# A planned instruction order for a Strassen matmul with GELU: two sets of planner constants changed

## The chip, the cores and the metric

The kernel runs on one core of a Trainium2 chip. The metric is the device time of one execution in microseconds. PE is the matmul engine, PEld its weight loads, DVE the vector engine, ACT the scalar engine, POOL the engine whose queue issues the loads here, SP the one whose queue issues the stores.

## The reference

Two float32 matrices of 4096 x 4096 are multiplied, and the approximate GELU is applied to every element:

```python
def reference(a, b):
    x = np.matmul(a, b)
    return 0.5 * x * (1 + np.tanh(np.sqrt(2 / np.pi) * (x + 0.044715 * x**3)))
```

## The kernel before, in words

**The arithmetic.** The kernel multiplies in float16 with a Strassen-like scheme. A and B are cut into 2 x 2 quadrants ("11", "12", "21", "22"), and seven products P1 to P7 of sums of quadrants take the place of eight. Each half of the rows is worked in 4 blocks (`mb`) and each half of the columns in 4 (`nb`); a pair of blocks is one group, which makes 16 groups, 0 to 15. Within the products of many groups the scheme is applied once more: a product is then cut again into seven smaller ones with 256 columns (`part_pe`, line 950), where an uncut one has matmuls of 512 columns (`products`, line 558).

**What moves.** Raw B is loaded by `load_raw` and raw A by `turn_quad`, both on POOL's queue; the transfer also turns float32 into float16. A quarter-block of raw A is turned on DVE (`transpose`, line 435) and each of its rows is squared and summed on ACT (line 1201), since the kernel ends with a test on the size of its inputs; raw B is squared on ACT too (line 1235). The sums of B's quadrants are made on DVE (`combine2`, line 866), stored to DRAM as units (`k_unit`, 512 KB a quarter) and pieces of units (`k_piece`) on SP's queue, and fetched again on POOL's queue in later row blocks. So a made piece has a round trip: DVE, store, fetch, PE. Results leave PE's banks through ACT (line 963, 1155, 1161) or DVE additions (`add_bank`, line 1167; `add_part`, line 967), become GELU on ACT (`out_of`, line 1145) and are stored from small tiles `y`, of which there are 15. All DMAs of the planned part are issued at line 784. The row blocks of A change in three turns, in groups 3, 7 and 11; the last two share POOL's queue with fetches of units.

**Where the order comes from.** Group 0 (`first_group`) is written out by hand, and its DMAs are issued at lines 460 and 654. From group 1 on the kernel does not issue instructions as it goes. It adds each as an `Op` with a duration to a `Plan`: its engine, what it reads and writes, and for a transfer a `size`, taken from the table `MOVE`. `Plan.keys` gives each operation a due time from the work behind it on PE. `Plan.schedule` then walks through time with a model of the engines and of the transfers. PE takes its operations in the order in which they were added. Any other engine takes, whenever it is free, the ready operation that is due first. `Plan.next_move` lets the open transfers share one channel; a queue has at most `LANES` = 8 of them open. `Plan.emit` issues everything in the order of the planned starts. On the chip each engine runs its own list in that order, and semaphores hold an instruction until its inputs are there. The planned times themselves never reach the chip; they only set the order.

Two lines of the planner use what the change touches. A due time takes off the time of a transfer, and an operation that reads what a transfer brought is ready a little after it:

```python
    def latency(self, o):
        return 6.0 + 1.5 * o.size if o.size else o.dur
    ...
                late = 0.0 if s.eng == o.eng and not o.size else LAG
                if o.size and s.eng in ("DVE", "ACT"):
                    late += MARGIN
```

Of the kernel before, what the change touches and what calls it, by code (L numbers as in the profile page):

```python
# [64 lines left out]
    "SP": [(0.62, t) for t in (10.4, 11.2, 12.4, 13.6, 14.6, 15.4, 16.2)],  # L65
}
LAG = 0.2
MARGIN = 1.5
LANES = 8
MOVE = {"store": 1.33, "fetch": 1.42, "out": 0.66, "raw_a": 1.35, "raw_b": 0.68, "tiny": 0.2}  # L70
HEAVY = 1.8
COST = {
    "full": 0.861, "half": 0.876, "wide": 0.983,
# [56 lines left out]
class Plan:  # L130
# [70 lines left out]
    def schedule(self):  # L201
# [13 lines left out]
        def finish(o):  # L215
            for s in o.succ:
                s.left -= 1
# [3 lines that stand above are left out]
                s.ready = max(s.ready, o.end + late)  # L221
# [93 lines left out]
def half_path(  # L315
# [463 lines left out]
    def dma(queue, dst, src, r, w, what, **kw):  # L779
        eng = {"POOL": nc.gpsimd, "SP": nc.sync}[queue]  # L780
        weight = HEAVY if what == "unit" else 1.0
        if what == "unit":
            what = "fetch" if queue == "POOL" else "store"
        return plan.add(queue, COST[queue], lambda: eng.dma_start(out=dst, in_=src), r=r, w=w, size=MOVE[what],  # L784
                        weight=weight, **kw)
# [1099 lines left out]
```

## Time and profile before

| | before |
|---|---|
| time, median of 3 runs | 1508.8 us (1503.86, 1508.8, 1509.66) |
| profiled execution, its own time | 1503.99 us |
| its span, first to last instruction | 1502.3 us |
| busy: PE / DVE / ACT / POOL | 99% / 79% / 47% / 31% |
| matmuls | 9886 |
| mean granted matmul clock | 0.998 |
| moved by DMA, mean rate | 397.14 MB, 264 GB/s |
| median time to landing: unit fetched / tile out / unit stored | 7.1 / 7.7 / 8.3 us |

The span is what the profile sees, and the time of the same execution is 1.7 us longer. The busy shares are means over all groups. Group 0 and the groups of raw B (1 to 6) load from the inputs; from group 7 on B's sums are fetched. The spread of the three runs is 5.8 us, 0.4% of the time.

### The profile page before, as it was taken

To read this page: it belongs to the slowest core of one execution; us is meant where nothing else is said; L and a number is where in the kernel's file an instruction comes from. 1 tells how busy PE (TensorE), PEld (TensorE's weight loads), DVE (VectorE), ACT (ScalarE), POOL (GpSimd) and SP (SyncE) were. 2 spreads that over 40 slices of the span, in tenths; PEclk is the share of its full clock that TensorE was granted. 3 is DMA by queue.
4 is the path that set the end of the run, shared out by engine and by line. 5 is a ranking of instruction groups with operands and counts; after the bars stand their busy time and mean duration, and the time that the engine had idled before them with its cause. 6 is when DMAs were issued, how large, how long until landed. Compare 5 with 4: busy or idle time off the path is not lost.

```text
span 1502.3 us, 26267 instructions
## 1 busy us (share of the span) xinstructions
PE 1486.2 (99%) x9886; PEld 968.1 (64%) x9886; DVE 1192.5 (79%) x1458; ACT 711.2 (47%) x1611; POOL 464.4 (31%) x834
## 2 busy tenths in 40 slices
PE   9999999999999999999999999999999999999998
PEld 4444454444445546565665788887665778888886
DVE  2597667357689899887799999998699987879886
ACT  5445246365854455546663142436564234343333
POOL 7766341542105315212330212222231112321310
PEclk9999999999999999999999999999999999999999
DMA  9999799999879999978997776898998567988976
GB/s 177 196 207 224 137 282 328 276 287 259 238 252 238 286 360 243 316 211 276 254 321 278 274 249 220 316 306 204 280 294 313 179 248 260 350 305 281 355 266 226
DMA packets 203366, 397.14 MB, mean 264 GB/s; under 512 B 20576, under 2 KB 110944, under 8 KB 203232
## 3 DMA queue, kind: packets, MB, share of 16 engines
q0 software_dynamic: 141024, 238.08, 65.9%
q1 hardware_dynamic: 62064, 157.19, 27.6%
q8 instruction: 79, 1.29, 0.3%
q14 instruction: 55, 0.45, 0.1%
q10 hardware_dynamic: 144, 0.13, 0.0%
HBM read 321.92 MB, written 157.29 MB: 319 GB/s over the span
## 4 chain that ended last, share of the span: by engine, by line
PE 88%; DMA 7%; POOL 2%; DVE 1%; issue 1%; ACT 0%; DVEq 0%; POOLq 0%; ACTq 0%
PE acc L558 47%; PE acc L950 42%; DMA bR<-k_unit 2%; DMA stage<-in_a_dram 2%; DMA out_dram<-y 1%; POOL stage L460 1%; POOL bR L460 1%; DVE bR L866 1%; DMA k_piece<-bR 1%; DMA bR<-in_b_dram 1%; POOL aD L460 0%; DVE y L1167 0%; DMA aD<-in_a_dram 0%; ACT stage L469 0%; POOL bR L784 0%
## 5 line engine op out<-in xcount | busy, mean ns | idle before, releaser
L558 PE MATMUL acc<-bR,aT 128*128 128x512 f16 x1920 | 421.6, 379 | 6.6 <-DVE y L1167 3.5
L866 DVE TENSOR_TENSOR bR<-bR 128x2048 f16<-128x2048 f16 (+1 forms) x284 | 331.7, 1188 | 53.8 <-PE acc L950 24.7
L558 PEld LDWEIGHTS <-aT 128*128 128x128 f16 x1984 | 194.0, 98 | 235.0 <-issue 7.4
L784 POOL DMA_DIRECT2D bR<-k_unit x254 | 146.4, 579 | 593.6 <-PE acc L950 337.5
L950 PE MATMUL acc<-bR 128*128 128x256 f16 x2576 | 299.2, 273 | 0.0
L558 PE MATMUL acc<-bR,aD 128*128 128x512 f16 x1344 | 294.5, 379 | 0.0
L950 PEld LDWEIGHTS <-bR 128*128 128x128 f16 x2576 | 252.1, 98 | 31.5 <-issue 0.2
L558 PEld LDWEIGHTS <-aD 128*128 128x128 f16 x1440 | 140.8, 98 | 167.4 <-DVE aD L543 0.8
L1167 DVE TENSOR_TENSOR y<-acc,y 128x512 f32<-128x512 f32 x304 | 197.4, 684 | 58.3 <-PE acc L950 23.8
L784 POOL DMA_DIRECT2D bR<-in_b_dram x288 | 155.8, 547 | 250.7 <-PE acc L558 98.8
L963 ACT COPY y<-acc 128x256 f32<-128x256 f32 x220 | 81.8, 372 | 231.8 <-PE acc L950 231.6
L950 PE MATMUL acc<-bR,aT 128*128 128x256 f16 (+1 forms) x1536 | 181.9, 274 | 1.8 <-DMA bR<-k_unit 1.2
L1145 ACT ACTIVATE y<-y 128x512 f32<-128x512 f32 x192 | 115.5, 626 | 132.0 <-DVE y L1167 130.4
L950 PEld LDWEIGHTS <-aT 128*128 128x128 f16 x1536 | 150.1, 98 | 24.0 <-DMA bR<-k_unit 1.5
L1235 ACT ACTIVATE y<-bR 128x1024 bf16<-128x1024 f16 x128 | 130.3, 1052 | 58.2 <-DVE y L1240 49.8
L950 PE MATMUL acc<-bR,aD 128*128 128x256 f16 (+1 forms) x1040 | 124.5, 275 | 0.0
L950 PE MATMUL acc<-bR,stage 128*128 128x256 f16 (+1 forms) x1008 | 120.3, 274 | 0.0
L950 PEld LDWEIGHTS <-aD 128*128 128x128 f16 x1040 | 102.5, 99 | 15.0
L950 PEld LDWEIGHTS <-stage 128*128 128x128 f16 x1008 | 98.7, 98 | 16.7
L1240 DVE TENSOR_TENSOR y<-y 128x1024 bf16<-128x1024 bf16 x120 | 82.1, 685 | 22.9 <-ACT y L1235 21.5
L1201 ACT ACTIVATE y<-bR 128x512 f16<-128x512 f16 x128 | 80.5, 629 | 26.0 <-DMA bR<-in_a_dram 22.5
L866 DVE TENSOR_TENSOR bR<-aT 128x2048 f16<-128x2048 f16 x61 | 74.0, 1217 | 20.0 <-PE acc L558 16.7
(92 smaller groups left out, 1220.5 us busy)
## 6 DMA issues: line engine op xcount, KB each, us to landing
bR<-k_unit POOLq DMA_DIRECT2D x254, 512.0 KB, 7.1
out_dram<-y SPq DMA_DIRECT2D x251, 256.0 KB, 7.7
k_unit<-bR SPq DMA_DIRECT2D x112, 512.0 KB, 8.3
bR<-in_b_dram POOLq DMA_DIRECT2D x384, 128.0 KB, 7.0
k_piece<-bR SPq DMA_DIRECT2D x44, 512.0 KB, 5.1
bR<-k_piece POOLq DMA_DIRECT2D x40, 512.0 KB, 7.8
bR<-in_a_dram POOLq DMA_DIRECT2D x64, 256.0 KB, 7.9
stage<-in_a_dram POOLq DMA_DIRECT2D x48, 256.0 KB, 7.5
```

The costliest lines, as they stand in the source:

```text
L460: nc.gpsimd.dma_start(out=dst, in_=src)
L558: nc.tensor.matmul(acc, sa[:, j // 2, i * P : (i + 1) * P, j % 2], sb[:, j, :], start=start and j == 0, stop=stop and j == 3, skip_group_c ...
L784: return plan.add(queue, COST[queue], lambda: eng.dma_start(out=dst, in_=src), r=r, w=w, size=MOVE[what], weight=weight, **kw)
L866: nc.vector.tensor_tensor(out=dst, in0=xa, in1=ya, op=ALU.add if op > 0 else ALU.subtract)
L950: nc.tensor.matmul(PS[s][i][:, :] if wide else PS[s][i][:, w * HC : (w + 1) * HC], sa[:, j // 2, r * P : (r + 1) * P, j % 2], rhs(j, wide) ...
L963: act(cost, lambda: nc.scalar.copy(out=d, in_=x), [xt] if xt else [], [dt])
L1145: act("gelu", lambda: nc.scalar.activation(t, t, ACT.Gelu_apprx_tanh), [("f", f)], [("f", f)])
L1167: dve("add", lambda: nc.vector.tensor_tensor(out=sm(g), in0=bank(s, i), in1=sm(f), op=ALU.add), [("f", f)], [("f", g), ("p", s, i)])
L1201: act("weigh", lambda x=x, r=r, s=s, f=f: nc.scalar.activation(small[f].bitcast(F16)[:, : 2 * RUN], s[:, x, :], ACT.Square, accum_out=t[:, ...
L1235: act("square", lambda t=t, src=src: nc.scalar.activation(t, src, ACT.Square), [c(cx)], [("f", f)], slack=60.0)
L1240: dve("add16", lambda t=t, u=u: nc.vector.tensor_tensor(out=u, in0=u, in1=t, op=ALU.add), [("f", f)], [("f", e)], slack=60.0)
```

## The change

Two constants of the planner are other ones. Each transfer counts as 3% longer (all six entries of `MOVE`), and `MARGIN`, the extra time after which DVE and ACT may read what a transfer brought, goes from 1.5 to 2.0 us. No operation, no tile, no address and no code of the planner differs; what can differ is the order of the instructions on DVE, ACT and the queues of POOL and SP, from group 1 on.

```diff
 LAG = 0.2
-MARGIN = 1.5
+MARGIN = 2.0
 LANES = 8
-MOVE = {"store": 1.33, "fetch": 1.42, "out": 0.66, "raw_a": 1.35, "raw_b": 0.68, "tiny": 0.2}
+MOVE = {"store": 1.37, "fetch": 1.463, "out": 0.68, "raw_a": 1.391, "raw_b": 0.7, "tiny": 0.206}
 HEAVY = 1.8
```

## The prediction

> **What bounds the kernel now.** I read the busy line of the page first, then the waits of PE alone, then the chain of work that ended last around PE's longest waits, and last the transfers in windows.
>
> ```profile
> PE 1486.2 (99%) x9886; PEld 968.1 (64%) x9886; DVE 1192.5 (79%) x1458; ACT 711.2 (47%) x1611; POOL 464.4 (31%) x834
> ```
>
> PE is busy for 1486.2 of 1502.3 us, so 16.1 us are not matmul. Every other engine has room on average. The change can touch only those 16.1 us or add to them: the list holds the same matmuls in the same order, because PE's operations are taken in the order in which the program added them, whatever the planner's times.
>
> ```profile
> PE acc L558 <- DVE y L1167: 3.5, 2, 2.4
> PE acc L558 <- DMA bR<-k_unit: 3.1, 1, 3.1
> PE acc L567 <- DVE table L739: 1.5, 1, 1.5
> PE acc L950 <- DMA bR<-k_unit: 1.2, 1, 1.2
> PE acc L950 <- DVE y L1167: 0.5, 1, 0.5
> PE acc L593 <- DMA bR<-in_b_dram: 0.5, 1, 0.5
> PE acc L558 <- ACT y L576: 0.4, 1, 0.4
> PE acc L558 <- DVE aD L543: 0.3, 1, 0.3
> ```
>
> These are all of PE's waits: microseconds in total, how many, the longest. The rows of L567, L593, L576 and L543 (2.7 us) belong to the first group, whose order is written out and not planned; nothing in the diff reaches them. The last matmul ends at 1497.2 us by the timeline (a run of 13.98 us from 1483.24), so 5.1 us are the last activation, store and wind-down. What is left to the planner is 3.5 + 3.1 + 1.2 + 0.5 = 8.3 us: 4.0 us in which PE waits for DVE to empty a bank, and 4.3 us in which it waits for a fetched unit. 2.7 + 5.1 + 8.3 make the 16.1.
>
> The chain of work through the longest wait for a unit, and through the longest for DVE (start, us, what):
>
> ```profile
> 1028.17 1.13 DVE bR L866
> 1029.30 0.28 issue
> 1029.59 0.90 POOL bR L784 x2
> 1030.49 0.25 issue
> 1030.74 0.57 POOL bR L784
> 1031.30 10.11 DMA bR<-k_unit
> 1041.42 0.02 issue
> 1041.44 0.02 POOLq L784
> 1041.46 0.53 issue
> 1041.98 16.28 DMA bR<-k_unit
> 1058.26 0.04 issue
> 1058.31 1.89 PE acc L558 x8
> ```
>
> ```profile
> 487.75 7.28 DMA out_dram<-y
> 495.02 0.03 issue
> 495.05 0.02 DVEq L1167
> 495.07 0.04 issue
> 495.12 0.70 DVE y L1167
> 495.82 0.04 issue
> 495.86 1.02 PE acc L558 x4
> ```
>
> At 1058 a unit took 16.28 us from issue to landing, against a median of 7.1 for its row on the page, and POOL could issue it only when an earlier one had landed. At 496 DVE waited for a finished tile to leave, because the small tile that it wants to write was still being stored.
>
> **The change, part by part.** Nothing is added or removed on any engine; only the planner's picture of the future changes, and with it the order on DVE, ACT, POOL and SP.
>
> *Longer transfers.* A fetch goes from 1.42 to 1.463 in the planner's list, a store from 1.33 to 1.37, a tile out from 0.66 to 0.68. At most 8 transfers are open on a queue, so the planner sees the last of a full queue land 8 x 0.043 = 0.34 us later than it did. The due times on which it ranks move by 1.5 x 0.043 = 0.06 us only. This reorders where two candidates were nearly level, and nowhere else.
>
> Is 1.42 too short now? Two windows, each with the transfers' share and rate in its last two columns:
>
> ```profile
> 1138.70:1158.70 20.00, 20.00 (x110) 10.61 (x109) 17.87 (x22) 8.57 (x14) 2.63 (x5) 1.00 1.03 409
> 1031.00:1058.00 27.00, 24.20 (x144) 13.88 (x142) 15.85 (x23) 19.64 (x51) 9.20 (x17) 1.00 1.08 266
> ```
>
> Where only units and finished tiles move, 409 GB/s make 0.524 MB / 409 = 1.28 us for one unit: shorter than both lists. Ahead of the wait at 1058, where raw A is loaded too, the queues are as full (share 1.08) and move 266 GB/s, which would be 1.97 us for a unit: longer than both. So the new list is wrong by a little more in quiet stretches and right by a little more in the turns of A. I price it at the turns, where PE waits.
>
> [...]
>
> *Data usable half a microsecond later.* This holds for DVE and ACT behind a transfer, not for PE. It concerns the transposes of raw A (row L435), the squares of raw A and B (L1201, L1235) and the sums of fetched units (L866). The planner fills the half microsecond with another instruction where one is ready. The displaced one then runs up to one instruction later on the chip: 1.22 us behind a sum or a transpose, 0.68 us behind an addition from a bank, 0.82 us behind a square with its accumulator read on ACT. Its cover: the waiters for L435 are ACT, POOL, and PE's weight loads for 0.2 us in all, so no matmul now waits on a transpose; behind a displaced sum stands its store, and behind that a fetch. Queued behind the displaced instruction is only the rest of its own engine, with 310 us idle on DVE and 791 on ACT. I take nought for it, between -0.5 us a wait (DVE no longer stands idle for the transfer) and +1.22 us a place where cover is gone.
>
> *What becomes of the 8.3 us.* At 1058 POOL stands in order between raw loads, whose buffers come free only when L435 and L1201 have read them, and fetches. With those readers 0.5 us later in the plan and the queue 0.34 us longer, the fetch is ranked about 0.84 us better against the raw load; the wait of 3.1 becomes 2.3. Bounds: nothing gained, or all 3.1. The wait of 1.2 at 1411 hangs on a store and a fetch in a row (11.42 and 7.61 us in the chain), with PE next: I take 0.3 us off, the longer queue alone. The two waits of 3.5 us behind a tile's store lose 2 x 8 x 0.02 = 0.3 us. Sum: 0.84 + 0.3 + 0.3 = 1.4 us gained. SP's and POOL's issues (0.33 and 0.53 us each) are as many as before.
>
> **The time.** The profiled execution took 1503.99 us for its span of 1502.3. The runs shown are 1503.86, 1508.8 and 1509.66, so with the profiled one two lie near 1504 and two near 1509, and their middle is (1503.99 + 1508.8) / 2 = 1506.4, 2.4 above the profiled one. 1503.99 - 1.4 + 2.4 = 1505.0. Against the median of 1508.8, about 0.5% (7.5 us) is what a measurement of this kernel can tell from no change: faster is below 1501.3, slower above 1516.3.
>
> **The rivals.**
> - *All the planned waits go.* Fetches in the turns are ranked early enough, and DVE does other work instead of standing behind a store. Then 8.3 us go: 1506.4 - 8.3 = 1498.1. For it: the waits are few and short, and the two at 1058 and 1411 are both late transfers, which is what the change plans for. It is also the only reading under which the 5 us between the two kinds of runs, if late transfers make them, would shrink. Against it: 0.84 us of better rank does not outweigh a transfer of 16.28 us, and 4.0 us hang on small tiles of which there are no more than before. Chance 0.25.
> - *Raw loads ahead of fetches: slower.* Place: the turns of A in which units are fetched too, 690 to 800 us and around 1040. A raw half quadrant is four loads of 256 KB; at the 266 GB/s of the turn they take 4 x 0.262 / 266 = 3.9 us. If at a full queue such four get in ahead of the unit that PE needs next, that unit lands 3.9 us later. From two such places on it decides (7.9 us); three give 1506.4 + 11.8 = 1518.2. For it: POOL is in order and already waits 13.9 us for L1201 between 690 and 800; the raw loads are lengthened too, and are due earlier. Against it: the later readers of raw A hold the next raw load back. Chance 0.13.
> - *The round trip of a made piece: slower.* A sum on DVE, its store and its fetch follow each other, and at 1411 PE has no time to spare behind them. A sum displaced by a sum and an addition is 1.22 + 0.68 = 1.9 us late; six such trips without cover give 1506.4 + 11.4 = 1517.8. Against it: PE shows one such wait in 60 stored pieces. Chance 0.08.
> - *No order that matters changes*, because due times move by 0.06 us: 1506.4. Chance 0.10.
>
> **How the numbers follow.** The forecast has 0.44. Faster is the first rival, 0.25; slower the second and third, 0.21; the rest, 0.54, is the same within the bound. Both ends are unsure, so the range goes from the first rival's 1498 to the two slower ones' 1518, which leaves out their far halves, about 2 in 10. The likeliest case's own range is 1502 to 1510: the bounds of its three terms and the two kinds of runs.
>
> **What would show it.** Right: PE's busy time stays at 1486; its waits are the same two kinds, with 6 to 8 us in all in the planned part; a wait for k_unit near 1058 is still there and shorter. The first rival shows as planned waits under 2 us. The second shows as a wait of PE for k_unit of 4 us and more in 690 to 1130 with raw loads just ahead on POOL; the third as waits of PE for k_unit or k_piece behind L866 and a store, after 800 us. I am wrong if PE's waits are of a kind that the trace above does not show, or if matmuls themselves take longer.

## The result and the profile after

The changed kernel is slower by 0.87%: 1518.39 us, the median of eight runs (1513.15 to 1523.7), against 1505.35 us for the kernel before on the same chip (eight runs, 1500.54 to 1509.66). The ratio is 1.0087, with a 95% interval from 1.0061 to 1.0113. The profiled execution of after took 1515.43 us for a span of 1513.9 us, 11.6 us more than the span of before.

The engines do what they did. The busy line of the page of after:

```profile
PE 1489.0 (98%) x9886; PEld 968.6 (64%) x9886; DVE 1198.0 (79%) x1458; ACT 714.0 (47%) x1611; POOL 465.1 (31%) x834
```

The counts are the same, and so is PE's list, instruction for instruction. PE's busy time grew by 2.8 us. PE's waits grew more. Their view for after, without the rows of the first group (us in total, how many, the longest):

```profile
PE acc L558 <- DMA bR<-k_unit: 5.6, 2, 3.1
PE acc L558 <- DVE bR L866: 3.7, 1, 3.7
PE acc L950 <- ACT y L963: 3.3, 1, 3.3
PE acc L558 <- DVE y L1167: 1.9, 2, 1.1
...
PE acc L950 <- DVE bR L866: 0.7, 1, 0.7
```

All waits of PE add up to 19.6 us, against 11.0 before. Two of the large rows are of a kind that before does not have: a sum on DVE (L866, at 555 us) and a copy on ACT (L963, at 783 us). The wait for a unit at 1058 is 2.5 us instead of 3.1, the one at 1411 is gone, and a new one of 3.1 us stands at 1115.

The rest of the difference is the granted clock. Before ran at half clock for 3.41 us, behind its wait at 496. After does so for 10.24 us: 6.83 behind 555 and 3.41 behind 783 (both kernels without the stretch behind the last matmul). Four stretches of after by windows (stretch, length, then busy time and count of PE, PEld, DVE, ACT and POOL, the granted clock, and the transfers' share and rate):

```profile
550.32:553.73 3.41, 0.80 (x4) 0.28 (x3) 3.08 (x4) 2.19 (x3) 1.13 (x3) 1.00 1.02 419
553.73:557.15 3.42, 2.35 (x6) 0.84 (x6) 3.42 (x4) 0.00 (x0) 3.20 (x6) 0.50 1.05 338
...
779.01:782.42 3.41, 0.36 (x4) 0.18 (x2) 2.03 (x2) 0.75 (x3) 1.06 (x2) 1.00 1.04 410
782.42:785.84 3.42, 3.13 (x15) 2.16 (x15) 3.42 (x6) 3.30 (x10) 0.00 (x0) 0.50 1.01 412
```

In each pair PE has little to do in the first stretch (0.80 and 0.36 us busy), and the clock of the next one is 0.50. At half clock a matmul of 512 columns follows the one before it after 0.42 us (behind 555) and one of 256 columns after 0.21 us (behind 783 and behind before's 496). At full clock the same kernels take 0.22 and 0.11 us for it. From these steps I estimate the cost at 2.8 us behind 555, at 1.4 us behind 783, and at 1.6 us behind before's wait at 496. So the waits grew by 8.6 us and the half clock by 2.8 + 1.4 - 1.6 = 2.6 us. Together that is 11.2 of the 11.6 us.

**Where the wait at 783 comes from.** The timeline of ACT around it, after (start, us, what, and in brackets the idle time and who ended it):

```profile
776.02 0.63 ACT L963 COPY y<-acc 128x256 f32<-128x256 f32 x2
781.67 0.63 ACT L1201 ACTIVATE y<-bR 128x512 f16<-128x512 f16 x1 [5.02 <-DMA bR<-in_a_dram]
...
782.30 0.63 ACT L963 COPY y<-acc 128x256 f32<-128x256 f32 x2
```

The same place before:

```profile
767.96 0.63 ACT L1201 ACTIVATE y<-bR 128x512 f16<-128x512 f16 x1 [2.55 <-DMA bR<-in_a_dram]
...
774.59 0.37 ACT L963 COPY y<-acc 128x256 f32<-128x256 f32 x1 [0.37 <-PE acc L950]
775.47 0.37 ACT L963 COPY y<-acc 128x256 f32<-128x256 f32 x1 [0.50 <-PE acc L950]
```

ACT stands for 5.02 us at a square of raw A whose data land at 781.5 us, and the two copies that free PE's banks are behind that square in its list; they start at 782.30, when it is through. In before the squares stand ahead of the copies too. There the load landed at 767.8 us, and the copies waited for PE, not PE for them. The last load of raw A was issued 7.3 us later (766.4 against 759.1) and took 15.1 us instead of 8.7. Four fetches stand earlier on POOL's queue than in before: one has got ahead of the half quadrant before it, two in among that one's loads, and one ahead of the last half quadrant itself. That they are what made it late is read from the order; it was not tried.

**Where the wait at 555 comes from.** The timeline of DVE in group 5, after:

```profile
537.84 6.90 DVE L866 TENSOR_TENSOR bR<-bR 128x2048 f16<-128x2048 f16 x6 [0.79 <-DMA bR<-in_b_dram]
...
550.65 0.69 DVE L1240 TENSOR_TENSOR y<-y 128x1024 bf16<-128x1024 bf16 x1 [0.52 <-ACT y L1235]
551.26 6.89 DVE L866 TENSOR_TENSOR bR<-bR 128x2048 f16<-128x2048 f16 x6
```

The same six sums before:

```profile
544.45 6.89 DVE L866 TENSOR_TENSOR bR<-bR 128x2048 f16<-128x2048 f16 x6
```

The sums that PE needs begin at 551.26, 6.8 us later than in before. The first of them reads a load that landed at 549.2. Ahead of them DVE and ACT take turns at the squares of raw B, and before those stands an earlier block of six sums. The raw B quadrants that feed this place land later than in before: the first of its batch was issued at 485.8 instead of 482.2 us, and two of its loads, the second of them the last, landed at 537.6 and 549.2 instead of 526.9 and 541.3. The first eight loads of the batch overwrite a buffer that a sum in group 4 reads. That sum runs 6.0 us later than in before (first line before, the others after):

```profile
477.97 1.22 DVE L866 TENSOR_TENSOR bR<-bR 128x2048 f16<-128x2048 f16 x1
...
479.13 0.69 DVE L1257 TENSOR_REDUCE stat_b<-y 128x16 f32<-128x512 bf16 x1
...
484.01 1.21 DVE L866 TENSOR_TENSOR bR<-bR 128x2048 f16<-128x2048 f16 x1
```

In after a statistics operation of raw B (lines 1255 to 1257) is on DVE in its place, and by the instruction lists another sum and three additions have come ahead of it too. Five of the loads behind the eight were then overtaken by eight others with the same due time. Of the kernels below (without e8_doses, whose order is planned anew) only e3_groups1to6 and e6_after_square have this exchange in their lists, and only these two have the wait at 555. This beginning of the chain is read from the lists; it was not tried by itself.

**Where the wait at 1115 comes from.** Two steps of the chain of waits, after:

```profile
1099.49 15.34 DMA bR<-k_unit
1114.83 0.04 issue
1114.87 3.18 PE acc L558 x14
```

In before this fetch was issued at 1090.4 us and took 7.6 us. Here it was issued 9.1 us later and took twice as long.

### The profile page after: what moved, and what is told of

It is laid out like the page before. It is cut to its first block, busy times and chain, and to the rows that moved or that the text cites. A ratio compares the mean times of both kernels' runs of the same rounds, so it can differ in the third digit from the quotient of the medians.

```text
span 1513.9 us, 26246 instructions
## 1 busy us (share of the span) xinstructions
PE 1489.0 (98%) x9886; PEld 968.6 (64%) x9886; DVE 1198.0 (79%) x1458; ACT 714.0 (47%) x1611; POOL 465.1 (31%) x834
## 5 line engine op out<-in xcount | busy, mean ns | idle before, releaser
L866 DVE TENSOR_TENSOR bR<-bR 128x2048 f16<-128x2048 f16 (+1 forms) x284 | 331.1, 1188 | 48.6 <-PE acc L950 21.3
L963 ACT COPY y<-acc 128x256 f32<-128x256 f32 x220 | 81.5, 372 | 225.1 <-PE acc L950 220.9
L967 DVE TENSOR_TENSOR acc<-acc,y 128x256 f32<-128x256 f32 x220 | 85.0, 424 | 12.0 <-ACT y L963 5.6
L1161 ACT COPY y<-acc 128x512 f32<-128x512 f32 x84 | 48.4, 588 | 97.1 <-PE acc L558 58.8
```

Of the source, the lines that this page charges most:

```text
L866: nc.vector.tensor_tensor(out=dst, in0=xa, in1=ya, op=ALU.add if op > 0 else ALU.subtract)
L963: act(cost, lambda: nc.scalar.copy(out=d, in_=x), [xt] if xt else [], [dt])
L967: dve("part", lambda: nc.vector.tensor_tensor(out=d, in0=xa, in1=ya, op=ALU.add), [xt, yt], [dt])
L1161: act("copy", lambda: nc.scalar.copy(out=sm(f), in_=bank(s, i)), [], [("f", f), ("p", s, i)])
```

## The experiments

Ratios are against the kernel before on the same chip, with a 95% interval. The medians of before were 1507.44 us beside the first four runs, 1506.1 beside the next four and 1506.18 beside the last four.

**One constant at a time.**

```diff
# e1_margin
-MARGIN = 1.5
+MARGIN = 2.0
# e2_moves
-MOVE = {"store": 1.33, "fetch": 1.42, ...
+MOVE = {"store": 1.37, "fetch": 1.463, ...
```

> Only the later use of landed data (MARGIN 2.0), transfers as before. Theory A (the time sits in three placed waits of PE, at 555, 783 and 1115 us of the changed kernel, with the half clock behind them; the one at 555 needs both constants, because raw B's loads must be late and be swapped): no wait over 2 us at 555, a wait of ACT and so of PE near 783 is possible; 1505 + 3 to 6 us, so 1508 to 1511. Rival B (the half microsecond alone does it all): all three waits, 1518. Rival C (no place: everything a little later everywhere): 1512, with no single wait that is new and over 2 us.

> Only the transfers 3% longer, MARGIN as before. Theory A: none of the three waits, 1505 within 3 us, the waits of PE in all within 2 us of the 11.0 of the kernel before. Rival B: 1505. Rival D (the longer transfers do it all): all three waits, 1518. Rival C: 1512, no single new wait over 2 us.

The longer transfers alone do nothing: 1507.98 us, 1.0004 [0.9986, 1.0023], waits of 10.2 us, and no half clock before the end (mean granted clock 0.999, against 0.998 in before with its one stretch). The later data alone cost as much as the whole change within the intervals: 1519.2 us, 1.0075 [1.005, 1.01]. My theory had 1508 to 1511 for it and missed. The waits of PE in e1_margin show one row that carries it:

```profile
PE acc L950 <- ACT y L963: 10.8, 3, 5.9
```

It has no wait at 555. Instead PE waits for ACT's copies at 778 (4.4 us) and at 1144 (5.9 us), in the turns of raw A in groups 7 and 11, and behind each the clock is at half for 3.41 us. So a part of the change costs by waits that the whole change does not have.

**New constants for some groups only.** An operation counts by its number in the plan:

```diff
+NEW = range(0, 2137)     # e3: groups 1 to 6; e4: 2137 on (groups 7 to 15); e5: 343 on (groups 2 to 15)
-                    late += MARGIN
+                    late += MARGIN if o.n in NEW else 1.5
...
-size=MOVE[what]
+size=(MOVE if len(plan.ops) in NEW else MOVE_WAS)[what]
```

> Both new constants for the operations of groups 1 to 6 alone, the old ones from group 7 on. Theory A: the wait at 555 is there (3 to 5 us, and 3.4 or 6.8 us at half clock behind it, 1.7 to 3.4 us more), those of 783 and 1115 are not; 1505 + 5 to 7 = 1510 to 1512. Rival C: 6 of 15 groups of a loss of 13 us spread evenly: 1510.5, but without a wait over 2 us that the kernel before has not.

> The other half: the old constants for groups 1 to 6, both new ones from group 7 on. Theory A: no wait at 555; the wait near 783 (3.3 us and 1.4 behind it, on ACT's copies) and the one near 1115 (3.1 us, on a fetched unit) are there: 1505 + 5 to 8 = 1510 to 1513. Rival C: 1513 without new waits over 2 us. Rival E (the later waits are only pushed on by what happened at 555): 1505, neither wait.

> Both new constants everywhere but in group 1, which keeps the old ones. Theory A2 (the loss is a few waits of PE that an early shift of the order sets up; the wait at 555 needs both constants from group 1 on): no wait over 2 us at 555, 5 to 7 us less than the changed kernel, 1512, and 1507 if the last raw half quadrant of the first turn with fetches then lands early enough. Rival C (the loss is spread over all groups): group 1 is one of 15, so about 1517 to 1518.

Groups 1 to 6 alone give the whole loss: 1520.48 us, 1.0094 [1.0065, 1.0124]. Their profile has the wait at 555 (3.7 us) and also the one at 783 (4.6 us), though from group 7 on the planner has its old constants. I had expected no wait at 783 there and 1510 to 1512 us, and missed both. Groups 7 to 15 alone cost nothing: 1504.43 us, 0.9997 [0.9973, 1.0022], without the waits at 783 and 1115. Theory A had them there and missed; rival E, which had neither and no loss, fits. In e3_groups1to6 a unit is waited for at 1117 as well (2.1 us). So neither wait comes from the constants at the place where it is seen. An order that has changed early goes on changing what follows.

With the old constants in group 1 and the new ones in all others, the wait at 555 is gone, and the kernel takes 1511.94 us, 1.0023 [0.9995, 1.0051]. The median is 6.4 us below after's, which fits the 6.5 us that the wait and its half clock cost in after (3.7 + 2.8); by the ratios it is 0.64%, or 9.6 us. The wait for ACT in group 7 remains, 3.1 us at 778.7, and so do waits for units at 1064, 1112 and 1425 (3.2, 2.2 and 2.9 us).

**The squares of raw A behind PE's copies.** In these kernels ACT's list alone differs, by the squares that are moved behind the two copies in a turn of raw A: one square of group 7 in after, and twelve squares of groups 7 and 11 in e1_margin.

```diff
# e6_after_square; e7_margin_squares has twelve such pairs
-        self.schedule()
+        self.schedule(); [setattr(self.ops[x], 'start', self.ops[y].start + 1e-4 * (k + 1)) for k, (x, y) in enumerate([(2422, 2470)])]
```

> The changed kernel with one swap in ACT's list: a square of raw A (L1201) that stands ahead of two copies (L963) comes behind them. Theory A2 (PE's wait at 783 is ACT standing in order behind a raw load that lands at 781.5, and nothing else): the wait of 3.3 us and the half clock of 1.4 us behind it go, 1518 - 4 to 5 = 1513 to 1514, all other waits stay. Rival F (PE waits there for something that is late anyway): the wait stays within 1 us, 1518.

> The kernel with MARGIN alone changed (1519), with the squares that stand ahead of copies put behind them in both turns that share POOL with fetches: twelve places in ACT's list, all other lists as they were. Theory A2: both waits (4.4 and 5.9 us, with 1.4 us of half clock behind each) go: 1519 - 13 = 1506, the time of the kernel before. Rival F: within 3 us of 1519. Rival G (the next raw loads, released by squares that are later, take the waits' place): 1512.

In e7_margin_squares the whole loss of the later data is gone: 1507.79 us, 0.9994 [0.997, 1.0017]. Of the 10.8 us of PE's waits for L963 this is left:

```profile
PE acc L950 <- ACT y L963: 0.5, 1, 0.5
```

This settles the margin alone: its cost was ACT standing at a square with PE's copies behind it.

In after the same move gave less: 1516.47 us, where 1513 to 1514 was expected, 1.007 [1.004, 1.01], and its interval overlaps after's. The wait for ACT is gone, but the next run of matmuls on line 558, which waits for nothing in after, now waits for a unit, as the timeline of e6_after_square shows:

```profile
781.76 2.54 PE L558 MATMUL acc<-bR,aD 128*128 128x512 f16 x11 [1.86 <-DMA bR<-k_unit]
```

In after this late unit was hidden behind the wait for ACT. Taking one away shows the other.

**What the half clock needs.** To see how much idle time brings the half clock, I added to the kernel before one to seven copies on DVE of an operand onto itself, ahead of every eighth product, so that PE waits for them. The order is planned anew with the copies in it, so the time of this kernel is no measure of anything else.

```diff
+    def dose(i, b_cell):
+        seen[0] += i == 2
+        k = seen[0] // 8 % 7 + 1 if i == 2 and seen[0] % 8 == 0 else 0
+        for _ in range(k):
+            plan.add("DVE", 0.6, lambda: nc.vector.tensor_copy(out=cell(b_cell), in_=cell(b_cell)), w=[c(b_cell)])
...
+        dose(i, b_cell)
```

> The kernel before with made waits: ahead of every eighth product's third tile DVE copies that product's operand onto itself, 1 to 7 times in turn, and PE must wait for it. Theory H (a wait of PE costs itself, and 1.7 us more where more than about 2 us of it fall into one period of 3.413 us of a fixed grid, since the clock is then granted at half for the next period): waits under 1.8 us are never followed by the half clock, waits over 3.8 us always, those between by where they lie. Rival I (the half clock follows the length of the wait alone): one length parts all waits, wherever they lie. The order is planned anew around the added copies, so the time is no test.

The half-clock stretches of a trace start on a grid of 3.413 us: those of after at 553.73 and 782.42 lie 228.69 us apart, 67 times 3.413, and in e8_doses the first, at 150.54, and the one at 1345.21 lie 1194.67 us apart, 350 times 3.413. I cut the trace along that grid and read PE's idle time in each period as its length less PE's busy time. Two pairs of periods, by windows of e8_doses:

```profile
447.50:450.92 3.42, 1.36 (x7) 0.39 (x4) 3.35 (x5) 0.79 (x2) 0.00 (x0) 1.00 0.70 261
450.92:454.33 3.41, 2.49 (x6) 0.87 (x7) 3.38 (x5) 0.00 (x0) 0.00 (x0) 0.50 0.00 0
...
1160.89:1164.30 3.41, 1.44 (x7) 0.68 (x7) 0.00 (x0) 3.25 (x10) 1.06 (x2) 1.00 1.03 414
1164.30:1167.72 3.42, 3.42 (x18) 1.57 (x16) 1.21 (x2) 0.36 (x2) 1.06 (x2) 1.00 1.04 416
```

An idle time of 3.42 - 1.36 = 2.06 us was followed by a period at 0.50. One of 3.41 - 1.44 = 1.97 us was not. All nineteen full-clock periods of this trace with 2.06 to 3.42 us idle were followed by half clock, and none with up to 1.97 was. In the traces of before, after, e1_margin, e7_margin_squares and e10_margin_raw_a the edge lies at the same place, between 1.97 and 2.00 us, where both outcomes were seen: 1.97 us was followed by half clock in e10_margin_raw_a, 1.97 us in e1_margin and 2.00 us in e7_margin_squares were not.

**The forecast's own place.** In before, the fetch that PE waits for at 1058 and two behind it are put ahead of five later-due loads on POOL's queue:

```diff
+        ... for k, (x, y) in enumerate([(3529, 3520), (3530, 3520), (3531, 3520), (3532, 3520), (3543, 3520)])]
```

> The kernel before with one edit in POOL's list alone: the fetch on which PE waits at 1058 (3.1 us) and the two fetches behind it go ahead of five loads that are due later and were issued first only because their buffers came free first. Theory J (that wait is made by POOL's order): the wait goes, 3.1 us and 1.7 more where it set off the half clock, 1506 - 3 to 5 = 1501 to 1503, a version that beats both. Rival K (the unit is late because raw A fills the queues, whatever the order): the wait stays over 2 us, 1506.

The wait of 3.1 us at 1058 is gone: the fetch lands at 1047.6 us, against 1058.3 in before, so POOL's order made that wait. Two stand there instead that before does not have, at 1069 and 1134:

```profile
PE acc L950 <- ACT y L963: 1.7, 1, 1.7
PE acc L950 <- ACT y L1161: 1.1, 1, 1.1
```

The time is 1503.46 us, 0.9981 [0.9963, 1.0000]: a gain at the edge of what was measured. It is the lowest median of all kernels here, and the only one whose interval does not reach above 1.

**Whose margin it is.** The margin of 2.0 for the readers of raw A alone, and for all other readers alone, each against the old list of transfers:

```diff
# e10_margin_raw_a
-                    late += MARGIN
+                    late += MARGIN if o.size == MOVE["raw_a"] else 1.5
# e11_margin_rest
-                    late += MARGIN
+                    late += 1.5 if o.size == MOVE["raw_a"] else MARGIN
```

> MARGIN 2.0 for the readers of raw A alone (transposes and squares), 1.5 for all others, transfers as before. Theory L (the half microsecond adds up along the chain load, readers, next load of a turn, and the last half quadrant comes late): it lands at 771 us and later against 767.8 in the kernel before, PE waits for ACT's copies near 778 and 1143 as with MARGIN alone, 1515 to 1519. Rival M (raw A comes late because the whole order around it is shifted, readers of units and raw B too): less than 2 us of waits there, 1506 within 3.

> The complement: MARGIN 2.0 for all readers but those of raw A. Theory L: no wait of PE for ACT's copies in the turns, 1506 within 3 us. Rival M: one or both of those waits, 1510 to 1519.

The waits for ACT's copies came as expected: 2.8 us at 784 and 3.6 us at 1146 with the readers of raw A, none over 0.5 us with the others. The rows, of e10_margin_raw_a and of e11_margin_rest:

```profile
PE acc L950 <- ACT y L963: 7.0, 3, 3.6
...
PE acc L558 <- DMA bR<-k_unit: 7.0, 2, 4.2
```

The second row was not expected: with the others, PE waits 4.2 us for a unit at 774, and the clock is at half for 6.83 us around it. The times did not follow the waits: 1509.8 us, 1.0022 [1.0003, 1.0042], where 1515 to 1519 was expected, and 1506.74 us, 1.0019 [0.9998, 1.0039]. Their sum, 0.4%, is less than e1_margin's 0.75%, whose two waits were each some 1.6 times as long (4.4 and 5.9 against 2.8 and 3.6 us). How the two parts lengthen each other's waits was not followed further.

**Both causes out.** The kernel with the old constants in group 1, and in it two squares of group 7 behind the copies:

```diff
# e5_groups2to15, and:
+        ... for k, (x, y) in enumerate([(2422, 2470), (2423, 2470)])]
```

> Both new constants from group 2 on (1511.9 with the old ones in group 1), and two squares of raw A put behind the two copies that PE needs in the first turn with fetches: the two large waits of the changed kernel are both taken away. Theory A2: 1512 - 3.1 - 1.4 = 1507.5; what is then left above the kernel before (2 us) are waits for fetches near 1112 and 1424. Rival N (the wait only moves to the fetch behind it, as when the square alone was moved in the changed kernel): 1510 to 1511.

It takes 1510.35 us, 1.0031 [1.0014, 1.0048], where theory A2 had 1507.5. The wait for ACT in group 7 is gone from its profile, but the time is not below that of e5_groups2to15 by anything that the intervals tell. So what the wait for ACT costs the whole change is read from its trace, 3.3 us and 1.4 of half clock; neither e6_after_square nor e12_both is faster than the same kernel with it by more than the noise. Late units remain, 2.9 us at 1059 and 2.2 us at 1105, and the tile's wait at 496 (2.2 us). The last 0.3% are not traced to one cause.

## Why the prediction was wrong, step by step

The forecast was 1505.0 us, no change; the result is 1518.4, slower. The few gains did not come by the steps that I gave for them, and the losses were on a side that I had priced at nought.

**"I take nought for it": the step that failed.** I judged the cover of a reader that starts half a microsecond later by who waits for L435 and L1201, and by ACT's mean idle time of 791 us. The row that mattered was not who waits for the square but what is queued behind it on ACT, where in after nothing else ran in the 5.02 us that the square waited. Two copies that PE needs stand there. Before's own trace had the place in view: the squares waited 2.55 us for the load and were through just before the copies. e7_margin_squares shows that this one neglect is worth all of e1_margin's 0.75%. In the whole change it stands beside the next step. What the forecast put at nought, with bounds of -0.5 us a wait and +1.22 us a place, is in after's trace 11.2 us of new waits and 4.2 us lost to the half clock.

**The price of a displaced instruction.** I bounded it by one instruction, at most 1.22 us. The operations that traded places were readers that free buffers, and loads queue for those buffers. Loads moved by whole places: raw B landed 10.7 and 7.9 us later, the last raw A 13.7 us later (781.5 against 767.8).

**"This reorders where two candidates were nearly level, and nowhere else."** It holds for the raw loads, and is not small. The raw loads of a batch have the same due time, so they are level, and eight of them went ahead of five others. e5_groups2to15 shows that the new constants in group 1 are worth some 0.6 of the 0.87% by the ratios, with intervals of 0.3 on either side of each. e3_groups1to6 and e4_groups7to15 show that such a choice lasts: new constants up to group 6 bring the wait at 783 in group 7, and new constants from group 7 on bring nothing. The forecast looked for each effect in the stretch where its wait was.

**The three terms of gain were mis-sized, and where one was near, that was luck.** They came to 1.4 us in the forecast and to 3.5 in the trace: 0.64 at 1058 (forecast 0.84), 1.23 at 1411 (forecast 0.3) and 1.6 at the two tile stores (forecast 0.3), with 1.6 us of half clock behind the latter besides. At 1058 the forecast had the fetch ranked better against the raw loads. POOL's list around it is the same in both kernels, five raw loads and then the fetch. The last two before and after:

```profile
1039.73 0.58 POOL L784 DMA_DIRECT2D bR<-in_a_dram  x1 [0.88 <-DMA bR<-in_a_dram]
1041.98 0.56 POOL L784 DMA_DIRECT2D bR<-k_unit  x1 [1.68 <-DMA bR<-k_unit]
...
1049.00 0.58 POOL L784 DMA_DIRECT2D bR<-in_a_dram  x1 [0.96 <-DMA bR<-in_a_dram]
1051.31 0.56 POOL L784 DMA_DIRECT2D bR<-k_unit  x1 [1.73 <-PE acc L558]
```

e6_after_square, with the lists of after but for one square, waits 3.07 us there, and 2.8 us at 1423, where after waits for nothing. Nor does the longer queue alone carry the tile stores: e2_moves waits 2.42 us at 496. That before's half clock would go with its wait was not in the sum at all, though the trace showed it. Against these gains stand new waits of 3.68 + 3.33 + 3.14 + 0.70 + 0.38 = 11.2 us and the 4.2 us lost to the half clock. The first group's waits, whose order is the same in both, differ by 0.8 us between the two executions.

**The longer transfers.** That a list 3% longer decides little was right; e2_moves shows no change alone. Whether 1.42 or 1.463 is nearer to the truth is left open by it. Beside the later data it may still matter, since the wait at 555 stands in after and not in e1_margin.

**The rivals.** "Raw loads ahead of fetches" had the place nearly right, 690 to 800 us, and the sign of the order wrong: fetches got ahead of raw loads, and the wait was for ACT. Its 1518 us agrees with the result as a number only. "The round trip of a made piece" was not seen: no wait for k_piece stands in after. "All the planned waits go" did not happen: those that before has lost 3.5 us of 8.3. The sign by which I said I would be wrong did appear: waits of a kind that the trace of before does not show.

## What to carry to other kernels

A constant in a planner's model is not priced by its own size. It decides between candidates, and early trades can move loads by ten microseconds several groups later; so compare the two orders themselves, or count the whole change as a new draw of small waits. Look for work that waits for a transfer and has PE's work queued behind it on the same engine, as ACT's copies stood behind the late square here: mean idle time of that engine is no cover (in before ACT stood idle for 791 us in all, and in after PE waited 3.3 us for it in one place), and moving only that work was enough to undo the 0.75% of e1_margin, though not to speed up the kernel with both changes, where other late data stood behind it. Price a wait of PE with the half clock behind it, an estimated 1.4 to 1.6 us a period here, if over about 2 us of it can fall into one period of 3.41 us (in e8_doses 2.06 us of idle time in a period brought it and 1.97 did not).

## What the runs showed of the hardware that I had not expected

In these traces the granted clock went by where a wait falls, not by its length alone. In before the wait of 2.36 us at 496 lies in one period and brought 3.41 us of half clock. The longer one of 3.10 us at 1058 lies across a boundary, 1.38 us in one period and 1.73 in the next, and brought none. The periods of both in before:

```profile
493.38:496.80 3.42, 1.06 (x6) 0.47 (x5) 1.68 (x2) 1.32 (x2) 1.63 (x3) 1.00 1.15 293
496.80:500.21 3.41, 3.41 (x18) 2.44 (x17) 3.41 (x5) 1.06 (x1) 1.09 (x2) 0.50 1.12 317
...
1053.17:1056.58 3.41, 2.03 (x10) 0.81 (x9) 0.00 (x0) 1.96 (x6) 1.06 (x2) 1.00 1.08 308
1056.58:1059.99 3.41, 1.68 (x8) 0.78 (x8) 0.00 (x0) 3.28 (x9) 1.06 (x2) 1.00 1.03 413
```

The wait of 3.14 us at 1115 in after, 1.79 and 1.36, brought none either. A period that is itself at half clock was followed by another with less idle time: 3.42 - 2.35 = 1.07 us in after, behind 555.

The grid lies differently in each trace: its first boundary is 1.86 us behind the start of the span in before and 0.77 in after. In e1_margin, where it is 3.12 us, the wait at 496 is 2.33 us long, with at most 1.72 us of idle time in one period, and brought none, where 2.36 us did in before. That one kernel's own wait costs the half clock in one execution and not in another is my inference from this; of each kernel one execution was profiled. This may be a part of the spread of the runs: of after's eight, the one at a mean clock of 0.999 took 1513.15 us and the one at 0.994 took 1519.95, though the order is not strict (0.995 stands beside 1514.66 and 1523.7).
